# A two-layer decoder on one core: attention by a written list, fills behind a copy, key pieces carried through the up projection, a close by tokens, another order of time mixing

## The chip, the cores and the metric

The kernel runs on one core of one Trainium2 chip. The metric is the device time of one execution in microseconds (us); the times are a median over runs, and one further execution was profiled. The engines are named as the profile names them: PE is TensorE (PEld its weight loads), DVE is VectorE, ACT is ScalarE, POOL is GpSimd, SP is SyncE, whose queue issues nearly all transfers.

## What is computed

The input x is 256 tokens of 1024 values, fp32. Layer 0 is causal attention with rotary positions and 16 heads of 64 (with 256 tokens there is one block, so the block-sparse choice of the reference chooses nothing else), then a gated feed-forward with a causal convolution of width 3. Layer 1 is RWKV-7 time mixing, a state of 64x64 for each head carried through the tokens, then another such feed-forward. A final norm follows:

```
for i in range(2):
    xn = rms_norm(h, norm_mix[i])
    h = h + (attention(xn) if i == 0 else rwkv7_time_mix(xn))
    xn = rms_norm(h, norm_ffn[i])
    gt = causal_conv3(xn @ w_gate) + conv_b
    h = h + (silu(gt) * (xn @ w_up)) @ w_down
return rms_norm(h, norm_final)

step of time mixing, for each head and token:
    sa = state @ -kk
    state = state * w + outer(sa, kk * a) + outer(v, k)
    y = state @ r
```

The time mixing is computed in parallel over the tokens: triangular matrices of 32x32, 64x64 and 128x128 tokens are formed and inverted step by step.

## The kernel before

**Layout.** Activations lie with the 1024 channels on partitions, as 8 tiles (kt) of 128 channels by 256 tokens. Dense products keep fp32 accuracy by halves: each operand is split into a rounded hi part and a lo part, and `mm3` (lines 165 to 169) issues three matmuls, hi·hi, hi·lo and lo·hi. Weights come from DRAM as pieces of 512 KB (128x1024) by SP's queue into four buffers `raw` (`pieces`, line 148); ScalarE casts the hi half and VectorE subtracts it to get the lo half (`split_act`, line 163). A piece lands in a pool `wp` of four, or, where it must stay longer, in the pool `b` of 17 blocks, in which nearly all large tiles lie. `issue_after` chains a transfer behind the transfer issued before it.

**Start and attention** (lines 252 and 267). `start` loads x by tiles, and after tiles 0, 2 and 4 a piece of the query weights; the constants `con` come last. `attention` is written as generators: `unit` projects queries, keys or values of one half of the heads, `soft` makes the scores and the softmax of two heads, `mix` multiplies by the values and splits the result into `oh` and `ol`; `weave` interleaves them, and the tile framework orders the engines as the program order goes. The output projection `out_proj` (line 223) is fed head pair by head pair; behind each pair of its output tiles (p = 0, 1, 2, 3) line 246 adds to h, and `finish` (line 181) makes hi (line 185), lo (line 186) and the squares of the next input.

**Feed-forward** (`ffn`, line 394). The up loop runs over 22 columns f; each takes two pieces (gate and up) and 48 matmuls of 256 columns, and then the gate's convolution and silu on VectorE and ScalarE. The down loop runs over 8 output tiles of 22 blocks each, 176 blocks (`blk`), a new piece every 8 blocks. In layer 0 it also carries `keys_ahead` (line 440): 8 pieces of the key weights wk of time mixing into pool `b` and one of wv, one at each `next(ahead)`, which are called at every second piece of the down loop:

```
if blk % 8 == 0:
    hi, lo = next(w)
    if blk % 16 == 8 and blk >= 16:
        next(ahead, None)
```

**Time mixing** (`rwkv`, line 448). All work is cut into named steps, and the string ORDER lists them in the order in which they are issued; within it PE, DVE, ACT and POOL execute in the written order, each waiting for its own data. Names that matter here: `vd`, `vhi`, `vlo`, `val` load, split and use pieces of wv; `wrd` and `wr` load and use wr (fp32, line 793); `gx` (line 757) transposes gathered 32x32 blocks into GX; `subst` (line 763) inverts them by 31 pairs of VectorE instructions (lines 767 and 769); `sc` (line 836) copies the turned result into the block-diagonal tiles DT; `back` and `back2` (line 827) transpose it into PN; `c32` (line 847) is the first product that reads PN, and `c64` the next level; `rkm`, `rkh`, `rkl` and `be` (lines 990 to 1003) belong to the bonus term; `recd` (line 971) multiplies r by its decay. The off-diagonal parts of DT, PN and of later tiles must be zero: steps named z (`zDT0`, `zPN`, `zmt`, `zRK0`...) are GpSimd memsets of 128x2048 (line 823). A fill has nothing to wait for but its tile, so it runs as soon as the tile's earlier contents were last read.

**Close** (`final`, line 1115). `rstd` makes the root of the norm for each token on partitions and spreads it over all partitions by two transposes (line 219); VectorE multiplies the five parts of hg by it (line 1120) and SP stores each (line 1121). The output has channels on partitions and is turned on the host.

Of the kernel before, what the change touches and what calls it, by code (L numbers as in the profile page):

```python
# [8 lines left out]
F32 = mybir.dt.float32  # L9
# [34 lines left out]
normed:0 vd:1 vd:2 mk:0 vd:3 normed:1 vd:4 mkh:0 mk:1 mkl:0 mkh:1 normed:6 key:2:0 vhi:1 mkl:1 key:1:0 normed:2  # L44
key:1:1 vhi:3 mk:2 key:0:0 normed:3 vhi:2 key:0:1 mk:3 key:2:1 mkh:2 normed:7 mkh:3 key:3:0 mkl:3 key:3:1 mv:7 mk:7
mvh:7 mkl:2 mkh:7 normed:5 key:2:2 mr:5 key:1:2 mk:5 key:1:3 mkl:7 mkh:5 mk:6 key:2:3 mkl:5 mkh:6 key:3:2 normed:4
key:3:3 mkl:6 key:0:2 mk:4 lora_end mkh:4 key:0:3 mkl:4 tanh mr:2 key:1:4 vlo:3 rates:0 mr:6 vd:5 rates:1 sig:0 mg:3
vlo:1 key:1:5 sig:1 rates:2 decays:0 wrd:0 key:0:4 rk:1 key:3:4 rk:0 key:3:5 decays:1 sig:2 key:3:6 key:3:7 rk:2
key:2:4 sq:3 key:2:5 decays:2 key:2:6 kkc:3 key:2:7 sums:3 kkc:2 mr:7 sq:2 key:0:5 rok:2 key:0:6 mr:4 mg:7 key:0:7
mr:0 key:1:6 kkc:0 mr:3 mg:0 key:1:7 sq:0 rok:0 rates:3 sq:1 mg:1 mg:2 gl:0 kkc:1 mvl:7 gl:1 mr:1 sig:3 gl:2 rok:1  # L50
gl:3 wr:0 mg:4 rk:3 mg:5 sums:1 decays:3 texp wr:1 powers:0 wr:2 wr:3 rok:3 powers:2 gl:4 wrd:1 rated:0 gl:5 facexp
mv:5 powers:3 rated:2 mg:6 powers:1 rated:3 gl:6 gl:7 mv:4 tsqrt vlo:2 wr:4 wr:5 rated:1 wrd:2 sqrt:1 sqrt:3 mvh:5
inv:3 gtc sums:0 inv:1 mvh:4 mv:0 spread:1 sqrt:0 mvl:5 mvh:0 inv:0 mvl:0 spread:0 dir:1 val:0:0 dirb:1 dir:0 sums:2
# [9 lines left out]
c32e:0 c32c:1:0 center:0:0 c32c:1:1 mv_:2 nE:0 nP:0 nD:0 c32e:1 mvp:2 c64:0 nP:1 nD:1 nE:1 c64:1 c64c:0 bm:2 vt:3  # L63
c64c:1 c64:2 vtc:3 center:1:0 gs:2 c64e:1 c64c:2 c64e:0 center:0:1 nG:1 c64:3 nG:0 me:3 c64c:3 zRK0 c64e:3 xs:3 zRB0
RK:0 nG:3 RK:1 zRK1 RKp:0 c64e:2 RKp:1 mv_:1 nG:2 rkm:1 RK:2 mvp:1 rkh:1 me:2 RKp:2 me:1 xs:2 rkl:1 be:1 xs:1
solve:0:1 rkm:0 bm:1 rkh:0 mv_:0 U:0:1 rkl:0 gs:1 carry:1 mvp:0 be:0 S:1 me:0 rkm:3 bm:0 rkh:3 carried:1 xs:0 zRB1
rkl:3 gs:0 solve:0:0 xa:1 solve:1:1 U:0:0 be:3 U:1:1 carry:0 bm:3 RB:3 S:0 gs:3 carried:0 RBp:3 RK:3 xa:0 RB:2 RKp:3
solve:1:0 RBp:2 out:0 U:1:0 out:1 out:3 out:2 RB:1 RB:0 RBp:1 outs RBp:0
# [27 lines left out]
class Trunk:  # L96
# [155 lines left out]
    def start(self):  # L252
        nc, a = self.nc, self.a
        self.table(AF.Sqrt, self.eps)
        nc.sync.dma_start(self.vec, a["vec"])
        self.begin("mix0", tok=True)
        self.wq = self.pieces(a["wqkv"], 24, fine=1)
        self.first = []
        for lo, n in ((0, 1), (1, 1), (2, 2), (4, 2), (6, 2)):
            nc.sync.dma_start(self.h[:, lo:lo + n], a["x"][:, lo:lo + n])  # L260
            for kt in range(lo, lo + n):
                self.finish(kt)
            if lo in (0, 2, 4):
                self.first.append(next(self.wq))
        nc.sync.dma_start(self.con, a["con"])

    def attention(self, nxt="ffn0"):
        nc = self.nc
        xhi, xlo = self.xhi, self.xlo
        V = self.b([128, 2, D], name="V")  # L270
        rope = Ring(self.b([128, 2048], name="rope"), 4, 512)
        smr = Ring(self.b([128, 1536], name="smr"), 2, 768)
        pr = Ring(self.b([128, 1536], name="pr"), 2, 768)
        ptb = [self.b([128, 5, 384], name="pts") for _ in range(4)]
        wq, first = self.wq, self.first
        qk = {}
        rt = cs = None

        def unit(g, t):
            ps = [self.acc([128, 512]) for _ in range(2)]  # L280
            for kp in range(4):
                hi, lo = first.pop(0) if first else next(wq)
                for k2 in range(2):
                    kt = 2 * kp + k2
                    w = slice(k2 * 512, k2 * 512 + 512)
                    for tt in range(2):
                        x = slice(tt * 128, tt * 128 + 128)
# [12 lines left out]
            if t == 0:  # L300
                qk[g] = self.b([128, 2, 4, S], name="qk")
            if t == 2:
                for tt in range(2):
                    nc.scalar.activation(V[:, tt, g * 512:g * 512 + 512], ps[tt], AF.Copy, scale=rt[:, tt:tt + 1])
                return
            rot = []
            for tt in range(2):
                src = ps[tt].rearrange("p (h d) -> p h d", d=64)
                at, bt = rope.next(), rope.next()
                av, bv = (z.rearrange("p (h d) -> p h d", d=64) for z in (at, bt))  # L310
                bc = lambda i, lo, n: cs[:, tt, i, None, lo:lo + n].to_broadcast([128, 8, n])
                nc.vector.tensor_mul(av, src, bc(0, 0, 64))
                nc.vector.tensor_mul(bv[:, :, :32], src[:, :, 32:], bc(1, 0, 32))
# [60 lines left out]
        z = []  # L374
# [837 lines left out]
```

## Time and profile before

| | us |
|---|---|
| median of 3 runs | 732.07 |
| lowest, highest | 728.87, 750.34 |
| the profiled execution | 724.09 |
| its span | 722.3 |
| mean granted TensorE clock | 0.994 |

The times are of whole executions; the span runs from the first to the last instruction of the profiled one, and every row below is of that one. Stages in it: attention and its output projection end at 129.05 us, the first up projection at 254.92, the first down projection at 320.84, time mixing with its output projection at 525.27, the second up projection at 651.06, the second down projection at 713.30, the close at 722.3. In the rows, `out<-in` are the program's names, `PE acc L169 <- DVE whl L163` is TensorE idle at line 169 until VectorE had made whl at line 163, and a granted clock of 1.00 is TensorE's full speed.

### The profile page before, as it was taken

The page shows a single profiled execution, that of the slowest core. Times are in us where ns is not written, and L with a number is a line of the kernel's source. Part 1 is how long each engine was busy: PE and PEld are TensorE (multiplying, and loading weights), DVE is VectorE, ACT ScalarE, POOL GpSimd, SP SyncE. Part 2 cuts the span into 40 slices and gives each one's busy share as a digit, 9 for nine tenths or more (in the row PEclk, how much of TensorE's full clock was granted, in tenths as well). Part 3 has the DMA queues.
Part 4 walks back from the last instruction along what each step waited for, and adds up shares of the span by engine and source line. Part 5 has one row for each costly group of instructions (what it writes and reads, how often), then busy time and mean ns, then how long its engine had stood idle before and what let it go on. Part 6 is the DMA issues. An engine that isn't in the chain of part 4 may idle for free.

```text
span 722.3 us, 14377 instructions
## 1 busy us (share of the span) xinstructions
PE 696.3 (96%) x5924; PEld 651.1 (90%) x5924; DVE 544.5 (75%) x929; ACT 399.7 (55%) x680; POOL 16.2 (2%) x18
## 2 busy tenths in 40 slices
PE   6999999999999999999999998999999999999995
PEld 4777778999999999998978877998999999999995
DVE  6898666688888875659988998856868888886552
ACT  6566675555555574433877355525456555555541
POOL 0000000000000000000002011100000000000000
PEclk9999999999999999999999999999999999999998
DMA  8744426255555577780112150300725555555531
GB/s 301 235 124 139 151 97 225 87 177 189 190 183 191 182 226 248 227 290 1 59 59 88 59 174 4 118 2 1 234 88 180 198 180 193 184 184 194 184 113 58
DMA packets 30737, 108.70 MB, mean 150 GB/s; under 512 B 3408, under 2 KB 4048, under 8 KB 30672
## 3 DMA queue, kind: packets, MB, share of 16 engines
q1 hardware_dynamic: 30672, 107.79, 45.6%
q8 instruction: 46, 0.75, 0.4%
q14 instruction: 19, 0.16, 0.1%
HBM read 106.73 MB, written 1.05 MB: 149 GB/s over the span
## 4 chain that ended last, share of the span: by engine, by line
PE 69%; DVE 13%; DMA 10%; ACT 4%; issue 3%; SPq 1%; DVEq 0%; ACTq 0%
PE acc L167 18%; PE acc L168 18%; PE acc L169 17%; DMA raw<-wk 5%; DVE whl L163 3%; ACT whl L163 2%; DMA raw<-wqkv 2%; DVE whl L767 2%; DVE GX L769 1%; DMA raw<-wgu 1%; PE acc L676 1%; PE acc L793 1%; PE pu L623 1%; PE pt L676 1%; PE pt L922 1%
## 5 line engine op out<-in xcount | busy, mean ns | idle before, releaser
L163 DVE TENSOR_TENSOR whl<-raw,whl 128x1024 fp32r<-128x1024 f32 (+1 forms) x182 | 220.5, 1217 | 89.2 <-ACT whl L163 89.0
L163 ACT CAST whl<-raw 128x1024 fp32r<-128x1024 f32 (+1 forms) x182 | 188.5, 1043 | 112.9 <-issue 51.4
L168 PE MATMUL acc<-xlo,whl 128*128 128x256 f32 x704 | 198.3, 282 | 0.0
L167 PE MATMUL acc<-xhi,whl 128*128 128x256 f32 x704 | 198.0, 281 | 0.0
L169 PE MATMUL acc<-xhi,whl 128*128 128x256 f32 x704 | 196.2, 279 | 0.0
L169 PEld LDWEIGHTS acc<-xhi,whl 128*128 128x128 f32 x704 | 133.4, 189 | 0.0
L168 PEld LDWEIGHTS acc<-xlo,whl 128*128 128x128 f32 x704 | 132.5, 188 | 0.2 <-DVE xlo L186 0.2
L167 PEld LDWEIGHTS acc<-xhi,whl 128*128 128x128 f32 x704 | 132.3, 188 | 0.2 <-ACT xhi L185 0.2
L169 PE MATMUL acc<-hh,whl 128*128 128x256 f32 x352 | 98.8, 281 | 2.1 <-DVE whl L163 2.1
L168 PE MATMUL acc<-hl,whl 128*128 128x256 f32 x352 | 99.0, 281 | 0.7 <-DVE hl L163 0.7
L167 PE MATMUL acc<-hh,whl 128*128 128x256 f32 x352 | 98.8, 281 | 0.0
L169 PEld LDWEIGHTS acc<-hh,whl 128*128 128x128 f32 x352 | 66.4, 189 | 2.5 <-DVE whl L163 2.5
L168 PEld LDWEIGHTS acc<-hl,whl 128*128 128x128 f32 x352 | 66.2, 188 | 0.9 <-DVE hl L163 0.9
L167 PEld LDWEIGHTS acc<-hh,whl 128*128 128x128 f32 x352 | 66.1, 188 | 0.0
L163 ACT CAST hh<-ftmp 128x256 fp32r<-128x256 f32 x44 | 17.9, 406 | 52.9 <-DVE ftmp L419 52.9
L167 PE MATMUL acc<-whl,xhi 128*128 128x512 f32 x96 | 39.0, 413 | 5.7 <-ACT whl L163 5.7
L168 PE MATMUL acc<-whl,xhi 128*128 128x512 f32 x96 | 39.1, 407 | 0.7 <-DVE whl L163 0.7
L169 PE MATMUL acc<-whl,xlo 128*128 128x512 f32 x96 | 38.7, 403 | 0.0
L412 DVE TENSOR_TENSOR gb<-acc,rs 128x512 f32<-128x512 f32 x44 | 30.4, 691 | 6.7 <-PE acc L169 1.7
L793 PE MATMUL acc<-xr,raw 128*128 128x256 f32 x128 | 30.1, 384 | 1.3 <-DMA raw<-wr 1.3
L793 PEld LDWEIGHTS acc<-xr,raw 128*128 128x128 f32 x128 | 23.7, 190 | 5.3 <-DMA raw<-wr 1.9
L167 PEld LDWEIGHTS acc<-whl,xhi 128*128 128x128 f32 x96 | 18.4, 193 | 11.0 <-ACT whl L163 6.0
(258 smaller groups left out, 1235.1 us busy)
## 6 DMA issues: line engine op xcount, KB each, us to landing
raw<-wgu SPq DMA_DIRECT2D x88, 512.0 KB, 3.8
raw<-wd SPq DMA_DIRECT2D x44, 512.0 KB, 4.6
raw<-wqkv SPq DMA_DIRECT2D x23, 512.0 KB, 4.5
raw<-wo SPq DMA_DIRECT2D x16, 512.0 KB, 4.3
raw<-wk SPq DMA_DIRECT2D x8, 512.0 KB, 4.4
raw<-wv SPq DMA_DIRECT2D x8, 512.0 KB, 4.8
raw<-wr SPq DMA_DIRECT2D x8, 512.0 KB, 3.6
l<-g SPq DMA_DIRECT2D x2, 512.0 KB, 7.2
```

The lines of the kernel that those rows point to most:

```text
L163: return self.nc.scalar.copy(hi, src), self.nc.vector.tensor_sub(lo, src, hi.bitcast(F32))
L167: mm(out, lhsT=lh, rhs=rh, start=start, stop=False, skip_group_check=True)
L168: mm(out, lhsT=lh, rhs=rl, start=False, stop=False, skip_group_check=True)
L169: mm(out, lhsT=ll, rhs=rh, start=False, stop=stop, skip_group_check=True)
L412: nc.vector.tensor_mul(g[:, :, 2:], ps, rs[:, None, :].to_broadcast([128, 2, S]))
L623: mm(ps[e % 2 * 64:e % 2 * 64 + 64, e // 2, tt * 128:tt * 128 + 128], lhsT=r[:, tt, e:e + 1].to_broadcast([128, 64]), rhs=ident, start=Tru ...
L676: mm(ps[e][:, i], lhsT=x[o, j, t], rhs=y[o, j, t], start=True, stop=True)
L767: nc.vector.tensor_mul(t, GX[:, 0, j + 1:, j:j + 1].to_broadcast([128, n, m]), X[:, j:j + 1, :m].to_broadcast([128, n, m]))
L769: nc.vector.tensor_sub(X[:, j + 1:, :m], X[:, j + 1:, :m], t)
L793: mm(open_["rec", p][:, t % 2], lhsT=raws["r", t][:, kt * 128:kt * 128 + 128], rhs=xr[:, kt], start=kt == 0, stop=kt == 7)
L922: mm(ps[:, c, k], lhsT=ms[q][k % 2][:, k // 2 * 2 + c], rhs=V[:, c, hs], start=True, stop=True)
```

## The change

Five things change together; what is computed, and the number of dense matmuls, stays.

1. Attention and its output projection are one set of named steps, issued in the order of a written list ORDER_A, as ORDER does for time mixing. The output projection runs joined with the last heads, with its tiles finished in the order p = 0, 3, 1, 2. Intermediate buffers go back to a list when their last reader is issued. `start` takes a fourth first piece, ahead of the constants.
2. In the first feed-forward seven key pieces are taken in the up loop (f = 1, 4, ..., 19), and the down loop keeps calls at blocks 40, 88 and 136.
3. The fills are grouped, and two groups begin with a GpSimd copy of one word of a tile that a VectorE step writes: DT, and a part of PN, behind GX (after `gx`); mts and RK[0] behind DT[0] (after `sc:0:0`).
4. ORDER is another list of the same steps (444 for 447, the grouped fills being fewer).
5. The close turns hg by 16 transposes to tokens on partitions, where the root is a factor for each partition; ScalarE and VectorE copy and multiply one token tile each, in three parts of 256, 256 and 512 channels, and six stores follow, one of them on ScalarE's queue. The output's layout is (128, 2, 1024).

```
-normed:0 vd:1 vd:2 mk:0 vd:3 normed:1 vd:4 mkh:0 mk:1 mkl:0 ...
-gc:3 wr:20 wrd:6 wr:21 tk:0:0 gates:0 bk:0:0 val:1:0 gc:0 zDT0 val:1:1 val:2:0 vhi:5 zDT1 val:2:1 val:3:0 vhi:4 zPN
-val:3:1 wr:22 vbc:0:1 vbc:0:0 wr:23 wr:24 wrd:7 rev:2 wr:25 vt:1 wr:26 wr:27 wr:28 vd:6 vlo:5 wr:29 wr:30 vlo:4 vd:7
-wr:31 td val:4:0 rev:3 vtc:1 recd:3 val:4:1 sc:0:2 sc:0:0 sc:1:1 vhi:6 val:5:0 sc:0:1 sc:0:3 sc:1:0 val:5:1 vlo:6
-vhi:7 recd:2 vt:0 sc:1:3 vlo:7 val:6:0 vtc:0 rkm:2 val:6:1 recd:1 rkh:2 val:7:0 recd:0 rkl:2 val:7:1 sc:1:2 back be:2
-vbc:1:1 zmt tk:1:0 vbc:1:0 tk:1:1 bk:1:0 back2 c32:0 bk:1:1 mv_:3 c32c:0:1 center:1:1 c32c:0:0 vt:2 c32:1 vtc:2 mvp:3
...
+normed:0 vd:1 vd:2 mk:0 vd:3 normed:4 vd:4 mkh:0 mkl:0 normed:7 ...
+rev:1 subst zDT wr:17 wr:18 tk:0:0 gates:2 bk:0:0 gates:3 gc:2 wr:19 gc:3 wr:20 wrd:6 wr:21 wr:22 tk:1:1 wr:23 bk:1:1
+wr:24 wrd:7 rev:2 val:1:1 val:2:0 vhi:4 val:2:1 val:3:0 vhi:5 val:3:1 wr:25 vbc:0:0 vbc:0:1 wr:26 wr:27 wr:28 vd:6
+wr:29 wr:30 wr:31 vt:0 vd:7 vlo:4 rev:3 vt:1 vtc:0 be:0 vlo:5 vtc:1 val:4:0 vhi:6 recd:2 val:4:1 rkm:2 vlo:6 rkh:2
+val:5:0 vhi:7 recd:3 val:5:1 rkl:2 vlo:7 be:2 td val:6:0 sc:0:1 sc:1:3 val:6:1 sc:1:1 sc:1:2 sc:0:2 val:7:0 back
+sc:0:3 val:7:1 sc:1:0 c32:1 sc:0:0 vbc:1:0 center:0:0 vbc:1:1 zmt c32:0 c32c:1:1 c32c:1:0 back2 vt:3 c32c:0:0 c32e:1
+vtc:3 c32c:0:1 mv_:3 center:1:0 nE:1 nP:1 c32e:0 nD:1 recd:1 c64:2 nE:0 nD:0 nP:0 c64:3 mvp:3 c64c:2 c64:0 ...
...
+ORDER_A = """
+q:0:0 q:0:1 q:1:0 q:1:1 q:2:0 wd:4 q:2:1 wd:5 q:3:0 wd:6 q:3:1 wh:4 wl:4 wh:5 wl:5 rstd rt ri texp wd:7 wd:8 q:4:0 cs
...
+rc:2:0 nm:0 q:14:0 wh:17 wl:16 tp:0:0 tp:0:1 tc:0:0 wl:17 wd:19 q:14:1 tc:0:1 wl:15 sc:1 wh:18 wd:20 mx:3 rp:2:1
...
+fa:1 lp:7:3 lp:5:1 ha:3 lp:6:1 fx:6 lp:7:1 fs:7 fl:6 fx:7 op:2:2 fa:7 fs:6 ha:1 op:3:2 fa:6 lp:4:2 fs:3 fl:7 fx:3
+lp:5:2 fa:3 fs:2 fl:3 fx:2 lp:6:2 fa:2 fl:2 lp:7:2 ha:2 fx:5 fx:4 fl:5 fs:5 fl:4 fs:4 fa:5 fa:4
 """
...
-            if lo in (0, 2, 4):
+            if lo in (0, 2, 4, 6):
                 self.first.append(next(self.wq))
...
+        with self.tc.manual_schedule(engines={ET.PE, ET.DVE, ET.Activation, ET.Pool}):
+            for step in ORDER_A.split():
+                name, *args = step.split(":")
+                if name == "fx" and not begun or name == "fs" and not begun:
+                    self.begin(nxt)
+                    begun = True
+                steps[name](*map(int, args))
...
             self.split_act(hh[f // 8][0][:, f % 8], hh[f // 8][1][:, f % 8], t)
+            if f % 3 == 1 and f < 20:
+                next(ahead, None)
...
-                    if blk % 16 == 8 and blk >= 16:
+                    if blk % 48 == 40:
                         next(ahead, None)
...
-        def zero(x):
-            return lambda: nc.gpsimd.memset(x, 0.0)
+        def zero(*xs, behind=None):
+
+            def step():
+                if behind is not None:
+                    w = self.wk.tile([128, 1], F32, name="word", bufs=1)
+                    nc.gpsimd.tensor_copy(w[:behind.shape[0]], behind)
+                for x in xs:
+                    nc.gpsimd.memset(x, 0.0)
+            return step
...
+            "zx": zero_x, "subst": substitute, "zDT": zero(DT[0], DT[1], PN[:32, :, 32:], behind=GX[:, 0, 0, :1]),
...
+            "zmt": zero(mts, RK[0], behind=DT[0][0:32, 0, 0:1]), "zRK1": zero(RK[1]), "zRB0": zero(RB[0]), "zRB1": zero(RB[1]),
...
     def final(self):
-        nc = self.nc
-        rs = self.rstd()
-        for lo, n in ((0, 2), (2, 2), (4, 2), (6, 1), (7, 1)):
-            o = self.hg[:, lo:lo + n]
-            nc.vector.tensor_mul(o, o, rs[:, None, :].to_broadcast([128, n, S]))
-            nc.sync.dma_start(self.a["out"][:, lo:lo + n], o)
+
+        nc, ET = self.nc, mybir.EngineType
+        o = self.b([128, 2, D], name="o")
+        ps = [[self.pu([128, 512]) for _ in range(2)], [self.acc([128, 512]) for _ in range(2)]]
+
+        def turn(half, tt):
+            for k in range(4):
+                nc.tensor.transpose(ps[half][tt][:, k * 128:k * 128 + 128],
+                                    self.hg[:, half * 4 + k, tt * 128:tt * 128 + 128], self.c("ident"))
+
+        with self.tc.manual_schedule(engines={ET.PE, ET.DVE, ET.Activation}):
+            turn(0, 0)
+            turn(0, 1)
+            r = self.rstd_tok()
+            turn(1, 0)
+            turn(1, 1)
+            for half, o0, n in ((0, 0, 256), (0, 256, 256), (1, 0, 512)):
+                p, f = slice(o0, o0 + n), slice(half * 512 + o0, half * 512 + o0 + n)
+                nc.scalar.activation(o[:, 0, f], ps[half][0][:, p], AF.Copy, scale=r[:, 0:1])
+                nc.vector.tensor_scalar(o[:, 1, f], ps[half][1][:, p], r[:, 1:2], None, op0=OP.mult)
+                (nc.scalar if half else nc.sync).dma_start(self.a["out"][:, 0, f], o[:, 0, f])
+                nc.sync.dma_start(self.a["out"][:, 1, f], o[:, 1, f])
```

## Rows read from the trace of the kernel before

**Rows 1.** The page, busy time of each engine, share of the span, instructions.

```profile
PE 696.3 (96%) x5924; PEld 651.1 (90%) x5924; DVE 544.5 (75%) x929; ACT 399.7 (55%) x680; POOL 16.2 (2%) x18
```


**Rows 2.** Stretches: start:end, us, busy us (instructions) of engines, granted clock, DMA, GB/s.

```profile
10.40:129.05 118.65, 114.78 (x684) 92.28 (x682) 93.71 (x181) 75.46 (x160) 0.43 (x2) 1.00 0.52 173
...
137.00:246.00 109.00, 109.00 (x928) 109.00 (x927) 90.52 (x135) 64.08 (x98) 0.00 (x0) 1.00 0.58 188
...
254.92:320.84 65.92, 63.16 (x530) 62.53 (x529) 42.63 (x52) 32.82 (x40) 0.11 (x1) 1.00 0.77 249
...
436.90:440.30 3.40, 3.40 (x58) 2.85 (x56) 3.33 (x6) 1.49 (x3) 0.00 (x0) 0.50 0.00 0
...
651.06:713.30 62.24, 62.24 (x531) 62.24 (x530) 31.07 (x39) 27.95 (x39) 0.00 (x0) 1.00 0.42 137
```


**Rows 3.** Waits in attention: us in total, times, longest.

```profile
PE acc L167 <- ACT oh L163: 2.4, 2, 1.3
```


**Rows 4.** Waits in the first down projection, same columns.

```profile
ACT whl L163 <- DMA raw<-wk: 19.3, 8, 4.4
...
PE acc L169 <- DVE whl L163: 2.1, 2, 1.1
```


**Rows 5.** Groups of instructions by line and form, VectorE, whole span: busy us, mean ns.

```profile
L163 DVE TENSOR_TENSOR whl<-raw,whl 128x1024 fp32r<-128x1024 f32 x180 | 219.1, 1223 | 88.0 <-ACT whl L163 87.8
```


**Rows 6.** Waits of TensorE in time mixing, columns as in group 3.

```profile
PE pt L847 <- DVE PN L827: 3.2, 1, 3.2
...
PE acc L793 <- DMA raw<-wr: 1.3, 1, 1.3
...
PE pu L860 <- issue: 0.5, 1, 0.5
```


**Rows 7.** Timeline around the fills: start, us, engine, line, instruction, idle before.

```profile
420.70 2.35 DVE L836 COPY sqr<-GX 32x512 f32<-32x512 f32 x4
...
426.07 1.23 DVE L738 TENSOR_TENSOR whl<-raw,whl 128x1024 fp32r<-128x1024 f32 x1 [1.37 <-ACT whl L734]
...
427.21 0.87 DVE L990 SCALAR_TENSOR_TENSOR rk<-Rt,vec,KE 128x256 f32<-128x256 f32 x2
...
429.21 0.69 DVE L998 TENSOR_TENSOR rkl<-rk,rkh 128x512 fp32r<-128x512 f32 x1
...
429.41 1.81 POOL L823 MEMSET mt<- 128x2048 f32 x1 [38.42 <-DVE Rt L971]
...
429.93 3.49 DVE L836 COPY sqr<-GX 32x512 f32<-32x512 f32 x1
...
431.16 1.80 POOL L823 MEMSET sqr<- 128x2048 f32 x1
...
431.18 1.04 PE L931 MATMUL pu<-con,KE 128*128 128x128 f32 x8
...
433.45 3.86 DVE L827 STREAM_TRANSPOSE PN<-GX 96x1024 f32<-96x1024 f32 x2
...
435.41 1.20 PE L847 MATMUL pt<-PN,sqr 32*32 32x32 f32 x64 [3.19 <-DVE PN L827]
```


**Rows 8.** Timeline of the close, same columns.

```profile
716.28 2.54 DVE L1120 TENSOR_TENSOR hg<-hg,pt 128x512 f32<-128x512 f32 x5 [0.53 <-PE pt L219]
716.99 2.57 SPq L1121 DMA_DIRECT2D out<-hg  x5
```


**Rows 9.** Timeline of a fill with other work beside it.

```profile
446.89 1.80 POOL L823 MEMSET sqr<- 128x2048 f32 x1 [13.93 <-PE pt L879]
...
447.73 0.68 DVE L901 TENSOR_REDUCE vm<-VB 128x8 f32<-128x512 f32 x1
```


**Rows 10.** Instructions of three lines: duration ns min/median/max, first and last start, forms.

```profile
L246 DVE TENSOR_TENSOR h<-h,acc x8: 677/682/689, 122.3 to 526.3; 128x512 f32<-128x512 f32 x8
...
L185 ACT ACTIVATE xhi<-h,vec x24: 492/506/512, 3.7 to 527.7; 128x256 fp32r<-128x256 f32 x24
...
L186 DVE SCALAR_TENSOR_TENSOR xlo<-h,vec,xhi x24: 471/482/526, 4.3 to 528.3; 128x256 fp32r<-128x256 f32 x24
```

More of the change, by code (lines that the diff above doesn't have):

```diff
@@ L49 @@
[L49 to L53, printed above, removed]
@@ L64 @@
[L64 to L68, printed above, removed]
+normed:0 vd:1 vd:2 mk:0 vd:3 normed:4 vd:4 mkh:0 mkl:0 normed:7 key:2:0 normed:1 key:3:0 vhi:1 mk:1 key:1:0 vhi:3
@@ L323, in soft, with load, step, hi @@
-        def soft(j):
+        oh = self.b([128, KT, S], F32R, "oh")
+        ol = self.b([128, KT, S], F32R, "ol")
+        pieces, raws, t, qk = dict(enumerate(self.first)), {}, {}, {}
+        place = ((0, 0), (0, 1), (1, 0), (1, 1), (0, 2), (1, 2))
+        def load(name, dram):
+            def step(i):
+                raws[name, i] = self.raw()
+                nc.sync.dma_start(raws[name, i], dram[i // 2][:, i % 2 * 1024:i % 2 * 1024 + 1024])
+            return step
+        def hi(name, own=KT):
+            def step(i):
+                w = (self.b if name == "o" and i >= own else self.wp.tile)([128, 2, 1024], F32R, name="whl")
+                nc.scalar.copy(w[:, 0], raws[name, i])
+                pieces[i if name == "q" else (name, i)] = w[:, 0], w[:, 1]
+            return step
@@ new lines, in turn, with turned, values @@
+        def turn(n, tt):
+            tp = t["rp", n, tt] = self.pu([128, 4, 128])
+            for j in range(4):
+                nc.tensor.transpose(tp[:, j], t["ro", n, tt][0][:, j * 128:j * 128 + 128], ident)
+            rope.append(t["ro", n, tt][1])
+        def turned(n, tt):
+            g, w = place[n]
+            if g not in qk:
+                qk[g] = self.b([128, 2, 4, S], name="qk")
+            nc.scalar.copy(qk[g][:, w, :, tt * 128:tt * 128 + 128], t["rp", n, tt])
+        def values(n, tt):
+            g = place[n][0]
+            nc.scalar.activation(V[:, tt, g * 512:g * 512 + 512], t["q", n][tt], AF.Copy, scale=t["r"][:, tt:tt + 1])
@@ L330, in soft, with masked @@
             for e, o in enumerate(half):
[L331 to L332 removed]
+                mm(sc[e][:, 1:], lhsT=q[o, 128:], rhs=k[o], start=True, stop=True)
+        def masked(j):
+            t["sp", j] = smr.pop(0)
+            sm = t["sm", j] = t["sp", j].rearrange("p (e t) -> p e t", e=2)
             for e in range(2):
[L334 removed]
@@ new lines, in attention, with out, added, next_hi @@
+        ps = {}
+        def out(k, p):
+            if k == 0:
+                ps[p] = self.acc([128, 2, S])
+            wh, wl = pieces["o", k]
+            for e in range(2):
+                f = slice((2 * p + e) * 128, (2 * p + e) * 128 + 128)
+                self.mm3(ps[p][:, e], wh[:, f], wl[:, f], oh[:, k], ol[:, k], k == e == 0, k == 7)
+        def added(p):
+            hp = self.h[:, 2 * p:2 * p + 2]
+            nc.vector.tensor_add(hp, hp, ps[p])
+        def next_hi(kt):
+            nc.scalar.activation(self.xhi[:, kt], self.h[:, kt], AF.Identity, scale=self.v(nxt, kt))
```

248 lines of the change are left out of this document (140 added, 108 removed).

## The prediction

> **What bounds the kernel now.** I read the page's busy times first, then busy time and granted clock by stage, then the waits of each stage that ended TensorE's idle time, and last the timeline where such a wait is long. TensorE is busy 96% of the span [rows 1]; the question for every part of the change is how much of the rest it takes away, since no matmul of the dense work is removed. In a dense stretch nothing else shows: 928 matmuls in 109.0 us, so 0.1175 us for each of 256 columns, with VectorE busy 90.52 us beside it [rows 2]. The gaps lie in four places. Attention and its projections: 118.65 us with TensorE busy 114.78, so 3.9 us idle; the largest listed part is the wait for the hi half of a mixed head, 2.4 us [rows 2, 3]. The first down projection: 65.92 us against 62.24 us of the second one, which does the same matmuls without key pieces beside it [rows 2]. Time mixing: waits of 3.2, 1.3 and 0.5 us, and behind the longest a stretch of 3.4 us at a granted clock of 0.50 [rows 2, 6]. The close: from the last matmul of the down projection at 713.3 to the end at 722.3, of which the last multiplications and their stores take what follows 716.28 [rows 8].
>
> **Key pieces moved from the down to the up projection.** In the first down loop ScalarE waits for the arrival of wk pieces 8 times, 19.3 us in all, up to 4.4 us at a time; the casts behind it are late and TensorE waits 2.1 us for lo halves of weights [rows 4]. The second down loop, where nothing is carried along, is the nearest row for the loop freed of them: 65.92 − 62.24 = 3.7 us. Three calls stay in the down loop, but far apart (blocks 40, 88, 136 of 176), so I take the whole 3.7; lower end 1.6, if each of the three still costs the 0.7 us which is a third of the listed 2.1, upper end 3.7. In the up loop seven pieces are added. Each brings one VectorE subtraction of 1.22 us [rows 5] and one cast on ScalarE, which has more room (busy 64.08 of the 109.0 us [rows 2]). Three columns hold 3 x 48 matmuls, 16.9 us of TensorE; VectorE uses 90.52/109.0 of that, 14.0, and with the piece 15.3. So 1.6 us of slack stay for every piece, and TensorE hides it. The pieces' transfers stand on SP's queue behind those of the gate and up weights, and wgu pieces behind them come 0.5 MB later: the stage moved data in 0.58 of the DMA engines' time [rows 2], room for one piece more in six. I cost the up loop at nothing; what happens if that cover fails is a rival below.
>
> **Fills behind copies, and the order around them.** The timeline shows the long wait entire [rows 7]. POOL fills mt from 429.41 and sqr from 431.16, 1.8 us each; VectorE's scatter copy of 32x512, issued at 429.93, lasts 3.49 us, while four like it took 2.35 together (0.59 each): it ends when both fills have ended, 2.9 us late. The transposes into PN (`back` and `back2`, 3.86 for the two) begin only then, and the first corner product c32 waits for the earlier one until 435.41. After the change both fills are issued behind a POOL copy of one word that depends on GX or on a scatter: the first group runs beside the substitution, the second after sc:0:0, the last scatter of the new order. A scatter can no longer meet one. Beside fills, row by row, other forms kept their length: the tensor_tensor at 429.21, which overlaps the start of the fill, took 0.69, and the tensor_reduce at 447.73 under the fill of 446.89 took 0.68 [rows 7, 9].
>
> How early c32 can start is set by two engines. TensorE: in front of the first c32 the new list has the same matmul steps and be:0 besides (four 128-column matmuls, 0.13 each by the eight in 1.04 us [rows 7], 0.5). The wait for the wr piece (1.3 [rows 6]) should go, because wrd:1 stands 24 steps ahead of wr:4 in the new list and 15 in the old. Its wait of 3.2 before 435.4 began at 432.2, so it is ready at 432.2 − 1.3 + 0.5 = 431.4. VectorE: in front of `back` the fill's 2.9 are gone; rkm:0 and rkl:0 come in (0.87 for the pair of multiplications, 0.69 as the 128x512 tensor_tensor at 429.21), sc:0:0, sc:1:0 and recd:1 go behind (0.59, 0.59 and, the same shape, 0.69) [rows 7]. From 435.4 that is 432.2, and 430.8 if the 1.4 us go that VectorE waited ahead of 426.07 for a cast of a wv piece. So a wait of 0 to 0.8 is left; I take 0.5, nearer the upper end, since the loads vd:6 and vd:7 stand no further ahead of `back` than before. Removed: 1.3 + 3.2 − 0.5 = 4.0 us, be:0 being work moved ahead and not added; ends 2.4 (the wait for wr stays) and 4.5.
>
> **The clock.** After the 3.2 us wait the clock granted is 0.50 for 3.4 us and 58 matmuls, the lower of its levels, 1.2 GHz [rows 2]; at 2.4 GHz they need half, so 1.7 us are lost. In attention, where the idle pieces are at most 1.3 us, it stayed at 1.00 [rows 2, 3]. With at most 0.8 us left I take the 1.7 as gained; ends 0 and 1.7. Behind c32, the 0.5 us wait of the second corner product [rows 6] has other steps ahead of it in the new list; I take its 0.5, ends −2 and 1.2, because the chain of products there is rearranged entire and no row shows the new order.
>
> **Attention by a written list.** Same instructions, so only the waits change: at most 3.9 us can be had [rows 2]. Walking the new list with each instruction's length, I find new waits: tp:0:0 and tp:1:1 stand closely behind the normalising nm:0 and nm:1 (0.6 and 0.8 us), and ha:2 is late at the very end: add, two hi, one lo are 0.68 + 0.50 + 0.50 + 0.48 = 2.2 us [rows 10], and the first up column covers it with the 12 matmuls of its first four tiles, 1.4, so 0.8 to 0.9. Together 2.3 with some 0.6 for the mixed heads; 2.9 of the 3.9 come back. I take 1.0; ends −3 (the list's covers fail twice over) and 3.9. The fourth weight piece ahead of the constants costs nothing, as the constants are first needed four pieces later.
>
> **The close by tokens.** The spread of the root over partitions (two transposes) and its five multiplications go, 2.54 us from 716.28, with five stores issued from 716.99 over 2.57 [rows 8]. In their place: transposes beside the sums, and three parts of two copies on ScalarE and VectorE at once, about 0.4, 0.4 and 0.7 long, as the 512-column add takes 0.68 [rows 10]. First store some 0.6 earlier, last 1.4 earlier; but the same bytes must leave, so between 0.3 and 1.5: I take 1.1. The sixteen transposes come where TensorE otherwise idles. The Trainium skill, "TensorE: Matmul & The Clock Gate", Part 4, says that transposes do not count as busy work for the clock; by it the last eight could run at 1.2 GHz, which would leave the gain near 0.8 instead of 1.1. No row of this kernel shows transposes alone long enough to tell.
>
> **Sum.** 3.7 + 4.0 + 1.7 + 0.5 + 1.0 + 1.1 = 12.0 us. The profiled execution took 724.1, so 712.1. The median shown stands 8.0 above it and the lowest of the runs 4.8; with the middle, 6.4, the forecast is 718. Two per cent, about what a measurement here can tell from no change, lies at 717.4.
>
> **Rivals.** *The lists' covers fail* (0.22): each new order brings as many waits as it removes. Then the down loop's 3.7, the clock's 1.7 and the close's 1.1 are left and half of the fill's 2.9: 8.0, so 722.5. For it: VectorE is busy 75% and the list leaves it little room in time mixing. Against: waits of the old order are few and each has its named cause.
> *More is gained than I count* (0.22): all 3.9 of attention, 4.5 at c32, 1.2 behind it: 3.7 + 4.5 + 1.7 + 1.2 + 3.9 + 1.1 = 16.1, so 708.0 in the profile and 713 to 714.5.
> *Slower* (0.08): in the up loop the key pieces arrive late, as in the down loop (19.3/8 = 2.4 us, up to 4.4 [rows 4]); the cast that waits for one holds ScalarE, behind it stand the gate's activations and the next casts, so VectorE loses its 1.6 us slack and TensorE waits. It decides once a piece costs TensorE 12.0/7 = 1.7 us; at 4.4 − 1.6 = 2.8 it is 20 us, and the time 738. Against: by the buffers (four raw, four in wp) weights can be three pieces ahead of their use, and a piece holds 24 matmuls, 2.8 us.
> *The fills still collide* (0.08): `back2`, a transpose, stands 1.4 us behind sc:0:0, under the second fill of 3.6. No row has a transpose beside a fill, so between nothing and 2.5 us late; by the list c64 needs it about 6 us behind c32, so at most 2 reach TensorE, perhaps with the 1.7 of the clock: 720 to 722. The Trainium skill, "SBUF — State Buffer", Who interferes with whom, says that copies, casts and tensor_scalar can lock the ports shared with GpSimd for a whole instruction and that a tensor_reduce never does; the rows agree for the copy and the reduce, and it does not list the transpose.
> The forecast itself has 0.40, with 711 to 725 for its own range.
>
> **Range and chances.** 706 to 730 takes in the forecast, the first two rivals, the fourth, and the bounds of the unknown costs; the slower case and the ends beyond are left out. Faster by over 2%: the second rival and half of the forecast, 0.43. Slower by over 2%: the third at its worst and disturbances I do not see, 0.05. Within: 0.52.
>
> **What would show it.** The first down projection at about 62.3 us with hardly a wait on lo halves; the up loop at 0.1175 us a matmul throughout; no scatter copy over 0.7 us and c32 four us earlier without a stretch at 0.50 behind it; attention's idle time between 2 and 4 us; the last store issued within 4.5 us of the last matmul of the down loop. I am wrong if the up loop grows by over 2 us, if the new order of time mixing opens a wait elsewhere that costs more than 2, or if attention's end, where its last pair is finished late, idles longer than 2.

## The result, and the profile after

The changed kernel takes 719.43 us (median of 4 runs, 718.77 to 721.81) for 730.76 before (median of 4, 728.87 to 750.34): ratio 0.986, 95% interval 0.982 to 0.990. Forecast were 718 and a range of 706 to 730. The ratios leave out runs more than 1.5% above the fastest of a kernel, which drops many runs of the kernel before, so medians over all runs stand beside them.

The lines of the program have moved: in the changed kernel the split is L185, the three matmuls of `mm3` L189 to L191, c32 L966, the scatter copy L955, the transposes into PN L946, the fills L941. Busy times in the page after (answers to [rows 1]), then stretches by stage (to [rows 2]; columns as there): attention, first up projection, first down projection, a stretch behind c32, second down projection, close.

```profile
PE 699.7 (98%) x5938; PEld 659.4 (92%) x5938; DVE 539.6 (75%) x927; ACT 401.4 (56%) x683; POOL 17.0 (2%) x20
```

```profile
9.20:122.72 113.52, 111.89 (x687) 92.40 (x686) 94.72 (x184) 76.18 (x163) 1.77 (x2) 1.00 0.52 175
122.72:249.69 126.97, 126.97 (x1068) 126.64 (x1067) 108.85 (x163) 79.43 (x120) 0.00 (x0) 1.00 0.65 212
249.69:312.12 62.43, 62.43 (x529) 62.36 (x528) 35.37 (x45) 27.04 (x34) 0.12 (x1) 1.00 0.66 219
432.30:449.70 17.40, 17.40 (x154) 17.03 (x152) 9.87 (x16) 11.23 (x18) 3.86 (x3) 0.51 0.09 32
645.90:708.40 62.50, 62.50 (x530) 62.50 (x529) 31.05 (x39) 27.92 (x39) 0.00 (x0) 1.00 0.42 136
708.40:717.00 8.60, 2.90 (x26) 2.61 (x24) 2.12 (x5) 2.50 (x6) 0.00 (x0) 0.92 0.35 122
```

Three things are seen at once. Attention lost 5 us of its length. The first down projection has no idle time left in this profile. And behind c32 TensorE stands at half its clock for 17 us, where the profile before had 3.4 us of it.

The waits of TensorE over the whole span are few (columns as in [rows 3]); the 3.2 us ahead of c32 and the 1.3 for wr [rows 6] are gone, and so is the wait for the hi half of mixed heads [rows 3]. New is the wait of 1.6 us for `mlo`, the lo half of a mixed input, at 325 us; the two marked L979 and L982 lie behind c32:

```profile
PE acc L189 <- ACT whl L185: 6.3, 2, 5.9
PE acc L190 <- DVE mlo L640: 1.6, 1, 1.6
PE pu L979 <- issue: 1.1, 1, 1.1
PE acc L190 <- DVE whl L185: 0.8, 1, 0.8
PE pu L982 <- issue: 0.6, 1, 0.6
PE pu L440 <- DVE ol L447: 0.4, 1, 0.4
```

The fills (timeline of GpSimd, to [rows 7]) each begin behind a copy of one word of 0.17 to 0.19 us, the second group behind the last scatter:

```profile
386.98 0.19 POOL L939 COPY word<-GX 128x1 f32<-128x1 f32 x1 [36.07 <-DVE GX L869]
387.09 3.55 POOL L941 MEMSET sqr<- 128x2048 f32 x2
...
424.25 0.17 POOL L939 COPY word<-sqr 32x1 f32<-32x1 f32 x1 [32.72 <-DVE sqr L955]
424.36 1.80 POOL L941 MEMSET mt<- 128x2048 f32 x1
```

VectorE meanwhile: no scatter copy beyond 0.62 us. `back2` takes 2.26, the fill beside it for its first 0.7 us; but `back`, with no fill beside it, takes 2.35.

```profile
420.87 2.35 DVE L946 STREAM_TRANSPOSE PN<-GX 96x1024 f32<-96x1024 f32 x1
...
423.09 1.02 DVE L955 COPY sqr<-GX 32x512 f32<-32x512 f32 x2
...
425.43 2.26 DVE L946 STREAM_TRANSPOSE PN<-GX 32x1024 f32<-32x1024 f32 x1
```

The close (timeline, to [rows 8]): eight transposes at the end take 1.07 us, the first store is issued at 711.41, the last two at 712.82 and 713.31.

```profile
710.24 1.07 PE L1242 MATMUL acc<-con,hg 128*128 128x128 f32 x8
...
711.41 0.35 SPq L1255 DMA_DIRECT2D out<-o  x1
...
712.82 0.99 SPq L1256 DMA_DIRECT2D out<-o  x2
```

Stage lengths worked out of the first and last matmul of each stage, for the profiles that the text uses (us; "low" is the length of the stretch at 0.50 behind c32):

| profile | up begins | up 0 | down 0 | to c32 | c32 to output projection | low | close | span |
|---|---|---|---|---|---|---|---|---|
| before | 129.05 | 125.88 | 65.80 | 114.68 | 63.84 | 3.4 | 9.14 | 722.3 |
| before, again | 130.07 | 125.88 | 64.35 | 113.86 | 74.49 | 30.7 | 9.15 | 731.9 |
| changed | 122.72 | 126.98 | 62.43 | 111.15 | 70.36 | 17.1 | 8.67 | 717.0 |
| order and fills undone | 123.10 | 126.97 | 63.49 | 115.48 | 77.51 | 37.5 | 8.67 | 730.4 |
| fills alone | 122.67 | 126.97 | 63.21 | 111.44 | 71.94 | 20.5 | 8.68 | 719.8 |
| attention undone | 130.94 | 125.87 | 63.24 | 111.53 | 70.42 | 17.1 | 8.68 | 725.7 |
| keys undone | 122.91 | 126.97 | 65.15 | 111.34 | 69.68 | 17.1 | 8.69 | 722.2 |
| six dummies | 122.35 | 126.98 | 63.46 | 111.11 | 63.48 | 0 | 8.68 | 711.1 |
| ten dummies | 122.93 | 126.98 | 62.93 | 111.75 | 65.41 | 0 | 8.68 | 713.2 |

### The profile page after: what moved, and what is told of

Same layout as the page of the kernel before. It is cut to its first block, busy times and chain, and to the rows that moved or that the text cites. A ratio compares the mean times of both kernels' runs of the same rounds, so it can differ in the third digit from the quotient of the medians.

```text
span 717.0 us, 14391 instructions
## 1 busy us (share of the span) xinstructions
PE 699.7 (98%) x5938; PEld 659.4 (92%) x5938; DVE 539.6 (75%) x927; ACT 401.4 (56%) x683; POOL 17.0 (2%) x20
## 4 chain that ended last, share of the span: by engine, by line
PE 82%; DVE 12%; ACT 2%; DMA 2%; issue 1%; SPq 0%; DVEq 0%; ACTq 0%
PE acc L189 22%; PE acc L190 22%; PE acc L191 22%; PE acc L905 2%; DVE whl L879 2%; DVE GX L881 2%; DVE whl L185 1%; PE pu L735 1%; PE pt L788 1%; PE pt L728 1%; DVE whl L322 1%; PE pt L998 1%; PE pt L1060 1%; DMA h<-x 1%; PE pt L1041 1%
## 5 line engine op out<-in xcount | busy, mean ns | idle before, releaser
L185 DVE TENSOR_TENSOR whl<-raw,whl 128x1024 fp32r<-128x1024 f32 (+1 forms) x154 | 187.2, 1217 | 71.9 <-ACT whl L185 71.6
L185 ACT CAST whl<-raw 128x1024 fp32r<-128x1024 f32 (+1 forms) x154 | 159.7, 1041 | 87.9 <-issue 42.7
L189 PE MATMUL acc<-xhi,whl 128*128 128x256 f32 x704 | 198.1, 281 | 0.0
L191 PE MATMUL acc<-xhi,whl 128*128 128x256 f32 x704 | 197.7, 281 | 0.0
L189 PEld LDWEIGHTS acc<-xhi,whl 128*128 128x128 f32 x704 | 132.6, 188 | 0.2 <-ACT xhi L465 0.2
L191 PEld LDWEIGHTS acc<-xhi,whl 128*128 128x128 f32 x704 | 132.7, 189 | 0.0
L189 PE MATMUL acc<-hh,whl 128*128 128x256 f32 x352 | 99.0, 281 | 0.0
L191 PE MATMUL acc<-hh,whl 128*128 128x256 f32 x352 | 98.8, 281 | 0.0
L191 PEld LDWEIGHTS acc<-hh,whl 128*128 128x128 f32 x352 | 66.3, 188 | 0.0
L189 PEld LDWEIGHTS acc<-hh,whl 128*128 128x128 f32 x352 | 66.1, 188 | 0.0
L189 PE MATMUL acc<-whl,xhi 128*128 128x512 f32 x96 | 40.0, 416 | 6.3 <-ACT whl L185 6.3
L185 ACT CAST hh<-ftmp 128x256 fp32r<-128x256 f32 x44 | 17.8, 406 | 46.0 <-DVE ftmp L529 45.9
L315 ACT CAST whl<-raw 128x1024 fp32r<-128x1024 f32 x28 | 29.1, 1050 | 17.8 <-PE acc L191 11.9
L322 DVE TENSOR_TENSOR whl<-raw,whl 128x1024 fp32r<-128x1024 f32 x28 | 33.5, 1221 | 6.9 <-ACT whl L315 6.8
L191 PE MATMUL acc<-whl,xlo 128*128 128x512 f32 x96 | 38.1, 397 | 0.0
```

Source lines behind the costliest of these rows:

```text
L185: return self.nc.scalar.copy(hi, src), self.nc.vector.tensor_sub(lo, src, hi.bitcast(F32))
L189: mm(out, lhsT=lh, rhs=rh, start=start, stop=False, skip_group_check=True)
L191: mm(out, lhsT=ll, rhs=rh, start=False, stop=stop, skip_group_check=True)
L315: nc.scalar.copy(w[:, 0], raws[name, i])
L322: nc.vector.tensor_sub(w[1], raws[name, i], w[0].bitcast(F32))
```

## The experiments

The experiments ran on four chips, the kernel before beside each: its medians over all runs were 734.5 (beside itself again, order, attention and keys undone), 732.4 (fills alone, dummies, more dummies, one copy sooner), 734.1 (small dummies, six dummies, fills and dummies) and 734.1 (ten dummies), against 730.8 beside the changed kernel. A difference to the changed kernel's 719.43 can therefore be off by some 3 us; the stage lengths of the table do not hang on that.

**The kernel before, again** (no edit).

> The kernel before once more, for a second profile. Its profiled execution took 724.09 us, its timed runs 728.87 to 732.07. Theory A (the profiled execution had a matmul spacing 0.3% shorter than that of the changed kernel, and little time at the lower clock): this profile shows a span of 726 to 730, with longer stretches at a granted clock of 0.50 in time mixing or a longer spacing in the up projection of layer 1 than 125.8 us. Theory B (the profile is typical and only the timed runs carry more around it): span 722 to 723.5 again, the same stage lengths within 0.3 us.

Its runs took 731.87 to 738.21 (median 734.91), and 25 further runs beside them 721.4 to 741.6, with mean granted clocks from 0.996 (the fastest) to 0.970 (the slowest). Theory A held in its clock part: the span is 731.9, longer still than the 726 to 730 expected, and 30.7 us of it are a stretch at half clock; the second up projection is 125.9, not longer. Stretch behind c32, columns as in [rows 2]:

```profile
434.20:465.50 31.30, 31.30 (x518) 29.52 (x520) 16.08 (x22) 15.17 (x24) 5.35 (x3) 0.51 0.10 30
```

The span is 9.5 us longer, the part between c32 and the output projection 10.7. From this pair 27.3 us more at half clock cost 10.7, 0.4 us each, where 0.5 would be lost if TensorE never waited. The profile shown before was one of the kernel's best executions.

**Order and fills undone.**

ORDER is the old list, and the fills are apart again, without a word copied first:

```
-            ... "zDT": zero(DT[0], DT[1], PN[:32, :, 32:], behind=GX[:, 0, 0, :1]),
+            ... "zPN": zero(PN), "zDT0": zero(DT[0]), "zDT1": zero(DT[1]),
...
-            "zmt": zero(mts, RK[0], behind=DT[0][0:32, 0, 0:1]), ...
+            "zmt": zero(mts), "zRK0": zero(RK[0]), ...
```

> The changed kernel with the order list of time mixing and the separate fills of the kernel before; attention, key pieces and close as changed. By the two profiles the stretch from the end of the first down projection to the second up projection is 3.1 us longer in the changed kernel (207.7 for 204.6), because TensorE stands at a granted clock of 0.50 for 17 us behind c32: then this kernel takes 716.3, faster than the changed one by 3. Rival: the old order was shown at its best in the profiled execution, and the new order saves what the forecast said, 4.0 for c32 and more: then 723 or above. The scatter copy of 3.5 us and the wait of 3.2 ahead of c32 are back in either case.

727.07 median of 10 (717.68 to 732.23, clocks 0.995 to 0.971), ratio to before 0.997 (0.986 to 1.009), so not separated from it by the ratio, though its median lies 7.4 below the 734.48 beside it; 7.6 above the changed kernel by medians. The rival held: the 3 us that the new order seemed to lose came of comparing with the one good profile. The long scatter copy is back (durations in ns, min/median/max), and with it a wait of 3.9 us ahead of c32 (waits, columns as in [rows 3]):

```profile
L955 DVE COPY sqr<-GX x5: 611/623/3490, 413.4 to 423.6; 32x512 f32<-32x512 f32 x5
```

```profile
PE pt L966 <- DVE PN L946: 3.9, 1, 3.9
```

TensorE then stands at half clock for 37 us (columns as in [rows 2]):

```profile
429.50:466.50 37.00, 37.00 (x558) 34.88 (x554) 20.42 (x29) 16.27 (x26) 5.35 (x3) 0.50 0.11 35
```

**Fills alone**: the old order with the grouped fills.

ORDER is the old list with `zDT` right behind `subst` and `zmt` right behind `sc:1:2`, its last VectorE scatter.

```
-            "zmt": zero(mts, RK[0], behind=DT[0][0:32, 0, 0:1]), ...
+            "zmt": zero(mts, RK[0], behind=DT[1][64:96, 0, 64:65]), ...
```

> The changed kernel with the old order list of time mixing, in which only the fills are grouped and put behind copies as in the change (first group behind GX right after subst, mts and RK[0] behind the last VectorE scatter). Against the kernel with the old order and old fills (median 727.1 in its runs, 717.7 to 732.2): no scatter copy longer than 0.7 us and c32 about 2.9 us sooner. If the wait of 3.2 to 3.9 ahead of c32 is what starts the stretch at the lower clock, the stretch is near 17 us or less and the time 719 to 722; if the small products start it by themselves, it varies as before and the time is 727 - 2.9 = 724.

717.61 median of 4: 713.28 and 713.69 (clocks 0.999, 0.998), 721.52 and 722.13 (0.984); ratio 0.976 (0.966 to 0.985). c32 comes as early as in the changed kernel (111.44 for 111.15 in the table, 115.48 with the old fills). With four runs in two groups this is not told apart from 719.43: grouping the fills is worth all that order and fills bring together, and for the new list itself no gain is measurable. The wait for wr, which the new list removes, is still there (waits), but not the one of 1.6 us for `mlo`, which the new list opens; the two about cancel. No copy is long (durations in ns), and the two transposes, the first almost wholly beside the fill and the second without, take 2.08 and 1.94, together 4.05 from start to end, for 3.86 [rows 7] (timeline):

```profile
PE acc L908 <- DMA raw<-wr: 1.2, 1, 1.2
```

```profile
L958 DVE COPY sqr<-GX x5: 605/622/645, 412.7 to 421.5; 32x512 f32<-32x512 f32 x5
```

```profile
422.17 4.05 DVE L949 STREAM_TRANSPOSE PN<-GX 96x1024 f32<-96x1024 f32 x2
```

That the wait ahead of c32 starts the stretch is refuted as the only cause: here the wait is gone, and the profiled run has a stretch of 20.5 us all the same, as by its clock a second of the four.

**Attention undone** (`attention`, its output projection and `start` as before).

> The changed kernel with attention, its output projection and the start as before. By the profiles the first up projection begins 6.3 us earlier in the changed kernel: then this one takes 725.7. By the forecast's term for attention, 1.0: 720.4. The waits for the hi half of mixed heads (1.3 and 1.1 us) are back.

726.86 median of 10 (724.71 to 732.38), 7.4 above the changed kernel; ratio to before 1.001 (0.995 to 1.007). The waits of the old attention are back (waits of TensorE in attention, then stretches by stage, columns as in [rows 2]):

```profile
PE acc L189 <- ACT oh L185: 2.5, 2, 1.3
PE pu L342 <- DVE rope L337: 1.3, 1, 1.3
```

```profile
9.20:130.94 121.74, 116.39 (x687) 93.45 (x685) 95.27 (x185) 77.44 (x164) 1.09 (x2) 1.00 0.51 173
130.94:256.81 125.87, 125.84 (x1069) 125.58 (x1067) 107.54 (x161) 79.88 (x120) 0.00 (x0) 1.00 0.63 204
```

The first up projection, with the seven key pieces still in it (161 VectorE instructions), is back to 125.87: the 7.4 are what the new attention saves less what it costs there.

**Keys undone.**

```
-            if f % 3 == 1 and f < 20:
-                next(ahead, None)
-                    if blk % 48 == 40:
+                    if blk % 16 == 8 and blk >= 16:
```

> The changed kernel with all key pieces taken in the first down projection as before. The down projection is 65.9 again instead of 62.4, the up projection shorter by what the seven pieces cost there. If the up projection's 1.1 us more are half a matter of the execution (the second up projection was 0.3 longer too): 719.4 + 3.4 - 0.8 = 722.0. Rival: the pieces cost the up projection nothing: 722.8. Second rival: what is saved in the down projection is lost elsewhere (time mixing gets its keys no earlier): 719.4.

723.28 median of 10 (720.45 to 724.86), 3.9 above the changed kernel, ratio to before 0.993 (0.989 to 0.998). Not all of the 3.9 need be the keys': the profile has 3.4 us at half clock in its second up projection too, which is 2.2 us longer than the changed kernel's. First up and down projection:

```profile
122.91:249.88 126.97, 126.97 (x1068) 126.65 (x1067) 102.01 (x155) 72.40 (x114) 0.00 (x0) 1.00 0.56 183
249.88:315.10 65.22, 63.45 (x530) 62.83 (x529) 43.44 (x53) 33.59 (x41) 0.11 (x1) 1.00 0.77 251
```

The up projection is as long without the pieces as with them: they cost it nothing, and its extra 1.1 us come with the new attention. The down projection is 2.7 us longer than in the changed kernel's profile; but the other ten profiles with the changed loop show 62.9 to 63.5 us for its 62.4 (five of them in the table), so 1.6 to 2.7.

**Dummies**: spare fp32 products between the small ones, to learn what brings the clock down. `c32e` and `c64e` are the second products that follow `c32` and `c64`.

```
+        def warm(z, n):
+            for _ in range(n):
+                mm(z.rearrange("p a b -> p (a b)")[:, :256], lhsT=ident, rhs=self.con[:, :256], ...)
             q32[i] = self.pu([128, 16, 32])
+            warm(q32[i], (4, 2)[i])
...
```

One more stands ahead of each c64 and c64e.

> The changed kernel with 14 fp32 matmuls of 128x256 more, whose results nobody reads, between the small corner products (4 and 2 ahead of the two c32e, one ahead of each c64 and c64e). In the changed kernel TensorE's granted clock falls to 0.50 behind c32 for 17 us. Theory A: what brings the clock down is the run of 32x32 and 64x64 products itself, so wider work between them keeps it at 1.00 there; cost about 14 x 0.216 = 3.0 us, of which some 1.9 lie in waits of 0.76 and 1.29, gain up to 7: 714. Theory B: it is the two waits, 2 us in all, and the dummies fill them as well: the same. Theory C: the lower clock comes whatever TensorE does there: 719.4 + 1 to 3 = 721.

719.07 (718.77 to 722.16; clocks 0.998 but for one), ratio 0.980 (0.974 to 0.987). The clock stays at 1.00, so Theory C falls; the time hardly moves, because a dummy is two matmuls, of 0.216 us each in a row and some 0.31 each where one stands alone. Counted in the trace from their starts to the start of what follows, the 14 take 7.9 us and not the 3.0 I had reckoned. Stretch behind c32:

```profile
424.00:450.00 26.00, 26.00 (x541) 21.64 (x538) 17.37 (x26) 15.31 (x27) 9.13 (x6) 1.00 0.04 11
```

**More dummies** (27).

> As the kernel with dummies, but 27 of them (5 and 4 ahead of the two c32e, 1 ahead of each c32, 2 ahead of each c64 and c64e): 5.8 us of TensorE work that no result needs. Theory A: if 14 are too few to hold the clock and 27 hold it, this one is the faster of the two, 715; if 14 are enough, it is slower than the other by 2.5 to 3. Theory C: 723 or more.

724.63 (723.76 to 725.85): 14 were enough, and more only cost. By the same count the 27 take 13.8 us, 5.9 more than the 14, and the median is 5.6 higher.

**One copy sooner** (`c32c:0:1` ahead of `vtc:3`).

> The changed kernel with one step moved in the list: the second half of the copy behind c32 (c32c:0:1) ahead of vtc:3 on ScalarE, so that c32e:0 waits about 0.6 us less of its 1.29. Theory B (the waits bring the clock down): the stretch at 0.50 grows shorter or goes, 714 to 718. Theory A (the small products do): the stretch stays at some 17 us, 718.8, which is 0.6 less than 719.4.

720.87 (719.71 to 722.22), no gain. One wait shrinks from 1.1 to 0.8, another of 0.6 appears (waits), and the stretch keeps its 17.1 us (of which 17.0 here):

```profile
PE pu L979 <- issue: 0.8, 1, 0.8
...
PE pt L998 <- ACT zs L1002: 0.6, 1, 0.6
```

```profile
434.50:451.50 17.00, 16.70 (x140) 16.12 (x141) 9.54 (x16) 10.21 (x17) 3.35 (x2) 0.50 0.10 32
```

It speaks for Theory A, weakly, since of the 1.7 us of the two waits 1.4 are left.

**Small dummies** (14 of 128 columns).

> The changed kernel with 14 dummies of 128 columns instead of 256. In the kernel with dummies each took two matmuls of 0.216 us, 6.0 us in all, and the stretch at 0.50 was gone (719.1 for 719.4). Theory A and B alike, if half the width is enough: no stretch at 0.50 in time mixing and 3.0 us less than with the wide ones, 716. If it is not enough: a stretch of some 17 us is back and the time is 720 to 722.

716.61 (715.75 to 717.06, and one of 721.03 at 0.993): as forecast; the 14 now take 4.9 us, and by the mean clocks half the width still holds the clock in five of six runs.

**Six dummies, at c32e alone.**

> The changed kernel with six dummies of 128 columns, 4 and 2 ahead of the two c32e, none in the c64 stage: 1.3 us of work, at the places of the two waits (0.76 and 1.29). Theory B (the waits start the lower clock): it stays at 1.00, 714.5. Theory A (the small products): the clock falls a little later, in the c64 stage, for 14 to 17 us, and the time is 719 to 720.

Two runs at 712.87 and 712.99 (0.999, 0.997), four at 720.12 to 721.58 (0.985 to 0.990). Neither theory alone: work in the places of the two waits saves the clock at times, not reliably. The profile in the table is of the fastest run.

**Fills and dummies** (old order, grouped fills, 14 small dummies).

> The old order of time mixing with grouped fills behind copies (717.6 median, two runs at 713.3 and 713.7 with under 3 us at the lower clock, two at 721.5 and 722.1 with 23), and 14 dummies of 128 columns. If the dummies hold the clock in this order as well, every run lies at 713.5 + 1 to 3 = 714.5 to 716.5 and the spread is below 2 us; if not, two groups again, near 715 and 723.

721.19 median of 12 (719.53 to 723.72), every clock at 0.995 or above. The clock held, the time was missed by 5. In its profile the output projection comes 67.8 us behind c32, as with 14 dummies in the new order, but matmuls of the second up projection stand at 0.120 instead of 0.118 us:

```profile
519.07:647.10 128.03, 128.03 (x1069) 127.83 (x1068) 101.68 (x153) 71.92 (x112) 0.00 (x0) 1.00 0.54 173
```

The code of that stage is the same in all kernels, so these 2 us are not the work of fills or dummies; their cause stays open. Most of the rest is the price of the dummies: they take 4.9 us here as well, not 1 to 3, and 713.5 + 4.9 + 2 is 720.4.

**Ten dummies** (six at c32e, one ahead of each c64).

> The changed kernel with ten dummies of 128 columns: 4 and 2 ahead of the two c32e, one ahead of each of the four c64, none ahead of c64e. Six (c32e alone) gave 712.9 to 713.0 in two runs and 720.1 to 721.6 in four; fourteen gave 715.8 to 717.1 in five of six. If the clock is lost at the entry to the c64 stage (it fell at 432 to 435 in every profile of the changed order), four more there hold it in nearly all runs at a cost of 4 x 0.22 = 0.9: 714. If it is lost further on, two groups again, 714 and 721, with a median of 716 to 721.

714.78 (714.25 to 717.45, clocks 0.996 to 0.999), ratio to before 0.977 (0.972 to 0.982): by the mean clocks no run has a long stretch at half clock behind c32. It is faster than the kernel before, and its slowest run lies below the fastest of the changed kernel, 4.6 by medians, though on another chip. The ten dummies take 3.3 us.

```profile
424.00:450.00 26.00, 25.25 (x578) 23.39 (x580) 21.51 (x32) 17.65 (x31) 9.13 (x6) 1.00 0.14 44
```

## Why the prediction was right, and where it was not

The time came out as forecast, 719.4 for 718, but partly by luck. Profile against profile the change brought 5.3 us (724.1 to 718.8) and not 12.0: behind c32 6.5 us were lost where 2.2 were to be gained, and attention won more than its term. The base, in turn, was 5.7 too high. The two errors, 6.7 and 5.7, nearly cancelled.

**The base.** I put the profiled 724.1 in the middle of the runs by adding 6.4. That difference was no fixed cost around the execution: the profiled execution had 3.4 us at half clock behind c32, an ordinary one 30.7. The changed kernel's profile (718.8) stands at its median (719.4).

**Key pieces: right in kind, perhaps half in size.** 3.7 forecast; down projection 65.9 to 62.4, 3.5 by the two profiles. But these two are the extremes: the three profiles with the old loop show 64.35 to 65.80 us (mean 65.1), the eleven with the new one 62.43 to 63.52 (63.1), so about 2. The up projection takes seven pieces free of charge, as costed; the rival in which they delay it did not come.

**c32: right.** 4.0 forecast, 3.5 measured from the end of the down projection (114.68 to 111.15), 2.7 against the second profile of the kernel before (113.86) and 4.3 against the kernel with the old order. The cause of the larger part was the one named, the copy held by the fills. What I credited to the new list, the earlier wr load, is not seen: the wait of 1.3 went, but one of 1.6 for `mlo` came where 0.5 had been waited, and fills alone reach 111.44, within the 111.10 to 111.75 of the profiles with the new list.

**The fills collide no more: right.** No fill held a transpose for its length, for which no row had existed: beside one it took 2.08 and 2.26 us for 1.9, not 2.5 more. The 2.26 cannot be put down to the fill, as `back` took 2.35 in the same profile without one; what makes the transposes longer in the new list was not tested.

**The clock: the failed step.** "With at most 0.8 us left I take the 1.7 as gained" took the drop for the work of one long wait. The wait is gone, and the clock falls for 17 us all the same, in the profile of the changed kernel and, by their mean clocks (0.980 to 0.987), in its other runs. Ahead of the fall TensorE waits 0.6 and 1.1 us, less than the 1.3 in attention at which the clock stayed at 1.00. The long wait did play a part: in the three profiles that have it (2.2 to 3.9 us) the clock falls 0 to 1.5 us behind c32, in the five without it and without dummies 9 to 10 us behind. But something else then brings it down. In the two profiles compared this lost 6.5 us (63.84 to 70.36 from c32 on), and the 0.5 behind c32 with it; against an ordinary execution of the kernel before (74.49) it gained 4.1. What the 17 us cost can be estimated from the four profiles with dummies up to 14: less the dummies' own time they need 61.6 to 62.5 us from c32 on, some 8 less than 70.36 (7 if all of the six dummies lay in waits). The dummies show that what TensorE does in the corner stage decides: with ten spare matmuls the clock stays at 1.00. Whether the products of 32 to 64 rows or the short waits between them weigh more is not settled.

**Attention: mis-sized.** 1.0 forecast, 7.4 by runs, 6.3 by the two profiles (8.2 against attention undone). The step "2.9 of the 3.9 come back" failed: the new waits that I found by walking the list do not exist (one wait of 0.4 is listed), and the idle time is 1.6 for 3.9, less than the 2 to 4 that I gave as a sign. The part that the idle time could not show is larger: TensorE's busy time fell from 114.78 to 111.89 with the same instructions. In part this is what TensorE loses where it changes from one kind of matmul to another, which is mostly counted busy. From 12 us on the old order changes kind 70 times before the up projection, and the starts on either side of the changes lie 15.8 us apart in all; the new list changes 55 times, with 10.65 us. Above the usual spacing of each kind these are 6.8 us (2.1 of them listed as idle) and 3.5 (0.4), which accounts for 1.7 of the 2.9 us of busy time. No run varies the changes alone, so this is an account and not a proof. Some 1.2 us more seem to be the start, where full clock comes at 9.2 for 10.4; but with the new attention the up projection begins at 122.4 to 123.1 us whether full clock comes at 8.8 or at 11.8 (ten profiles; with 27 dummies all begins over 1 us later), and with the old at 129.1 to 130.9. I had capped the gain at the idle time, and it was no cap.

**The up projection: a cost not foreseen**, 1.1 us. It follows the new attention (126.97 with it, 125.87 without), not the pieces. My sign of 0.1175 us a matmul throughout was missed.

**The close: half right.** 1.1 forecast, 0.47 measured, the same in all profiles. First store 0.7 sooner after the last matmul (3.1 for 3.8), last issue finished 0.9 sooner (5.5 for 6.4), but the last bytes land 3.2 us behind it instead of 2.8. The last store is issued 5.0 us behind that matmul, not within the 4.5 that I gave as a sign. The lower bound, the bytes, was the better guide. The transposes were not slowed: eight in 1.07 us at a granted clock of 1.00, as eight other products of 128 columns in 1.04 [rows 7]. The loss that I had worked out from the Trainium skill ("TensorE: Matmul & The Clock Gate", Part 4) did not come; whether a longer run of transposes would hold the clock, no run here shows.

## What to carry to other kernels

Before a term for the clock is taken from one profile, look at the mean clocks of the timed runs: here one kernel spread over 20 us, and its mean clock with it from 0.996 to 0.970. Undo the suspected collision by itself before crediting a new order: grouped fills alone gave as much as fills and a searched list. And compare several profiles of the same stage: the first down projection differed by 1.5 us between two profiles of one kernel. Where the clock falls in a stage of small products, a few spare matmuls can be worth trying: here ten gained 4.6 us net of their own time. Idle time is no upper bound of what a better order of mixed shapes can gain.

## What was not expected

With the new attention each matmul of the first up projection takes 118.7 ns instead of 117.8, in every profile and in all of its length behind the first sixth (mean spacing of starts; 126.97 for 125.87 us), though its code is the same; the cause was not found. And one and the same kernel: the stretch at half clock behind c32 lasted 3.4 us in one profile and 30.7 in another.
